# A two-block transformer layer on one core: two buffers for the squares of the first norm, memory attention's keys and values in another pool, norm 2's statistics one step later

## The chip, the core and the metric

The kernel runs on one core of one Trainium2 chip. TensorE (PE) multiplies matrices, VectorE (DVE) and ScalarE (ACT) work on tiles, GpSimd (POOL) does a little of the same, SyncE (SP) issues nearly all transfers. Each engine executes its own instructions in the order in which the program holds them, and waits on semaphores for the others. The metric is the device time of one execution in microseconds (us). Of the kernel before, three runs have a median of 1642.4 us (1641.32 to 1644.54).

## The reference, cut to what matters

Two blocks over a sequence of 512 tokens with 1024 features, everything in float32.

The first block norms x, shifts and scales it by parameters made from a condition vector, and mixes gated linear attention and differential attention; then norm 2 and a gated feed-forward layer:

```python
sh1, sc1, gt1, sh2, sc2, gt2 = adaln_params(c, w_mod, b_mod)   # silu(c) @ w_mod + b_mod
px = project(modulate(x, norm1_g, sh1, sc1), w_in)             # rmsnorm(x) * (1 + sc1) + sh1
mix = concat([gla_merge(...), diff_merge(o, diff_norm_g)]) @ w_out
x = x + gt1 * mix
x = x + gt2 * swiglu(modulate(x, norm2_g, sh2, sc2), w_ffn_in, w_ffn_out)
```

The second block has a pooling and forgetting-attention mixer, attention over 256 memory rows, and a convolved feed-forward layer, each between a norm before and a norm after:

```python
x = x + rms_norm(merged @ w_mix_out, mix_post_g)
x = x + rms_norm(mem_attention(rms_norm(x, xa_pre_g), mem_n, w_xq, w_xkv, w_xo), xa_post_g)
x = x + rms_norm(conv_ffn(rms_norm(x, ffn_pre_g), w_up, conv_w, conv_b, w_down), ffn_post_g)
```

## The kernel before, in words

Features lie on partitions, tokens along the free dimension: X is 8 tiles (k = 0 to 7) of 128 x 512. A float32 product is made of three matmuls of a reduced format: every operand is split into a high part (hi, a cast) and a low part (lo, what the cast left over), and `mm3` (L196 to L198) and `tm_part` (L285 to L287) issue hi·hi, and the two mixed products. `wsplit` (L173) brings a weight tile: an SP transfer into the ring `wf` (2 buffers), the cast into `whi` on ACT (L187), the subtraction into `wlo` on DVE (L188; some on POOL). The feed-forward layers put some of these into memory of their own, named Fhi and Flo.

A scheduler places the instructions of each engine by a priority that counts up with the text; `tc.cur_priority -= n` lets an instruction go earlier, `tc.issue_after(i)` holds it behind instruction i. A tile from a pool waits until what lay at that place, a former buffer of the same tag or a pool that has been closed, is read for the last time.

Three places matter here.

The head. `normed_x` (L427) squares X: for each pair of tiles ACT squares the even one into t (tag sqt0, two buffers), DVE squares the odd one into u (L433, tag sqt1, `bufs=2 - j`, one buffer) and adds t (L434), and PE sums u over partitions (`sum_sq`, L313). `warm` (L488) puts matmuls of no use ahead of these sums: `WU` before the first, `WX` before each later one. Then come the root (L165 to L170), its broadcast (L332, L333), X times it (L441), and per tile `modulated`: hi on ACT (L381), the affine on DVE or POOL (L382), lo (L383). Between them PE makes the condition's parameters (`mod_tiles`, L353, L365). Queries and keys (s, 512 columns a matmul) and the values `gv` (272 columns) follow. `gd` (L1171) is a constant of 128 numbers for the differential attention's norm; it reads `cols`, a tile that SP brings. The context rows have a norm of their own: cX times its root (L424), then hc (L381 to L383).

Norm 2. After the out-projection, `norm2` (L1323) is a generator that runs between the matmul groups of the feed-forward layer, one `yield` for a group's quarter: `W4` steps before the second half of the tokens has its statistics (L313), then 3 steps until they are broadcast. X's first tiles get the projection added at L1343.

Memory attention. Keys and values, KV, lie in the pool `xp`, which is closed when the attention is done. `post` (L1434) writes the output projection into KV's place (L1438), norms it there (L1452) and adds it to X (L1453); `after` runs between matmul groups as norm 2 does, `rbp` is its broadcast root. The convolved feed-forward layer then takes the memory of the closed pool for Fhi, Flo, z and others: what is put there waits until KV has been read for the last time, at L1453. `hq` is a pool that stays open to the end.

Of the kernel before, what the change touches and what calls it, by code (L numbers as in the profile page):

```python
# [10 lines left out]
F32 = mybir.dt.float32  # L11
# [3 lines left out]
ALU = mybir.AluOpType  # L15
# [5 lines left out]
S = 512  # L21
TT = S // 128
CTX = 256
MEM = 256
# [22 lines left out]
QP = (0,)  # L47
Q3 = 0
MG = 1
WU, WX, WW = 15, 1, 5  # L50
MV, W0 = (0, 1), 1
XG = 9
ML = 0
W4, W5 = 1, 1
W1, W2 = 2, 2
X2 = (0, 2, 4)
XR, DR = (1, 3, 5, 7), (1, 3, 5, 7)
# [3 lines left out]
WO = 50  # L61
# [19 lines left out]
def kernel(ctx: ExitStack, tc: tile.TileContext, a: dict, out: bass.AP, stop=None):  # L81
    nc = tc.nc
    V, G, A, T = nc.vector, nc.gpsimd, nc.scalar, nc.tensor

    def f32(ap):
        return ap.bitcast(F32)
# [20 lines left out]
    def mis(dt=F32):  # L107
        return ps.tile([128, 512], dt, tag="mis", name="mis")
# [18 lines left out]
    def col(name, i):  # L127
        o = COLS[name][0] + i
        return cols[:, o:o + 1]
# [180 lines left out]
    def sum_sq(pt, sq, start, stop):  # L310

        for t in range(sq.shape[-1] // 128):
            ins = T.matmul(pt[:, 32 * t:32 * t + 32], sq[:, t * 128:(t + 1) * 128], ones, start=start and t == 0, stop=stop,  # L313
                           skip_group_check=True).ins
        return ins

    def fm_stats(pool, sq, name):

        n = sq.shape[-1] // 128
        pt = mis()  # L320
        sum_sq(pt, sq, True, True)
        return rms(pool, pt, n, name)

    def rms(pool, pt, n, name):
        return rsqrt(pool, pt[:, :32 * n].rearrange("p (t o) -> p t o", o=32)[:, :, 0], n, 1.0 / D, name)

    def bcast(dst, r):

        n = r.shape[-1]
        pb = mis()  # L330
        for t in range(n):
            T.matmul(pb[:, t * 128:(t + 1) * 128], r[:, t:t + 1].to_broadcast([128, 128]), ident, start=True, stop=True)  # L332
        return A.copy(dst, pb[:, :n * 128]).ins  # L333
# [43 lines left out]
    def modulated(t, hi, lo, sc, sh, pool, tag, eng=G):  # L377

        n = t.shape[-1]
        u = pool.tile([128, n], F32, tag=tag, name=tag, bufs=2)  # L380
        hi_at[0] = A.activation(hi, t, AF.Identity, scale=sc, bias=sh).ins  # L381
        eng.tensor_scalar(u, t, sc, sh, ALU.mult, ALU.add)  # L382
        return V.tensor_tensor(lo, u, f32(hi), ALU.subtract).ins  # L383
# [5 lines left out]
    with tc.tile_pool(name="st", bufs=1) as st, tc.tile_pool(name="st2", bufs=2) as st2:  # L389
# [37 lines left out]
        def normed_x(x):  # L427

            pt = mis()
            for k in range(0, KT, 2):  # L430
                t, u = (st2.tile([128, S], F32, tag=f"sqt{j}", name="sqt", bufs=2 - j) for j in range(2))
                A.activation(t, x[:, k], AF.Square)
                V.tensor_tensor(u, x[:, k + 1], x[:, k + 1], ALU.mult)  # L433
                V.tensor_tensor(u, u, t, ALU.add)  # L434
                with tc.issue_after(warm(WU if k == 0 else WX)):
                    last_warm[0] = sum_sq(pt, u, k == 0, k == KT - 2)
            yield
            rb = st.tile([128, S], F32, tag="rbx", name="rbx")
            yield bcast(rb, rms(st, pt, TT, "x"))
            for k in range(KT):  # L440
                V.tensor_tensor(x[:, k], x[:, k], rb, ALU.mult)  # L441
                if k == 1:
                    yield
            yield
# [26 lines left out]
        def hidden(k0):  # L471
            affine(scx, "norm1_g", 8, 0, k0, 2)
            for k in range(k0, k0 + 2):
                ins = modulated(X0[:, k], hhi[:, k], hlo[:, k], scx[:, k:k + 1], mods[:, k, 0:1], st, "mx", V if k in MV else G)
            return ins
# [8 lines left out]
        def warm(n, ins=None):  # L484

            for _ in range(n):
                with (tc.issue_after(ins or last_warm[0]) if ins or last_warm[0] else ExitStack()):
                    last_warm[0] = T.matmul(pq[:, :128], ident, ident, start=True, stop=True).ins  # L488
            return last_warm[0]
# [10 lines left out]
        hid = hidden(0)  # L500
# [667 lines left out]
        mnl = mlo[:, 4:8].rearrange("p k (u t) -> p (k u) t", u=2)  # L1168

    gd = midp.tile([128, 1], F32, name="gd")  # L1170
    V.tensor_scalar(gd, col("diff_norm_g", 0), 0.8, None, ALU.mult)  # L1171

    def mem_in(k):
        m = ap2.tile([128, MEM], F32, tag="mk", name="mk")
# [116 lines left out]
    sp = ctx.enter_context(tc.tile_pool(name="sp", bufs=2))  # L1291
# [31 lines left out]
    def norm2(x, y):  # L1323
        for _ in range(W4 if x else W5):
            yield
        r = fm_stats(sp, sqs[:, x:y], "n2")
        for _ in range(3 if x else 1):
            yield
        bcast(rb[:, x:y], r)
        for k in range(KT):  # L1330
            if k % 2:
                yield
            t = sp.tile([128, S // 2], F32, tag="n2t", name="n2t")
            V.tensor_tensor(t, X[k][:, x:y], rb[:, x:y], ALU.mult)
            modulated(t, h2[0][:, k, x:y], h2[1][:, k, x:y], sc2[:, k:k + 1], mods[:, 24 + k, 0:1], sp, "n2u")

    with tc.tile_pool(name="wo", bufs=1) as wo:
        keep = kept(wo, (0, 1, -1, -1, -1), 0)
        have = {(m, 0): wsplit(a["w_out"][m].rearrange("p k m -> p (k m)"), 1024, None, keep()) for m in (3, 4)}
        for m, (p, whi, wlo) in enumerate(parts):  # L1340
            mm3(p, whi[:, 896:1024], wlo[:, 896:1024], mhi[:, 7], mlo[:, 7], False, True)
        for m, (p, _, _) in enumerate(parts):
            V.scalar_tensor_tensor(X[m], p, mods[:, 16 + m, 0:1], X[m], ALU.mult, ALU.add)  # L1343
        for m in range(len(parts)):
            add_sq(X[m], m, 0, S)
        fm(a["w_out"], range(3, KT), KT, lambda k: mhi[:, k], lambda k: mlo[:, k], accs, ev_out, HALVES, after=norm2,
           keep=keep, have=have)
# [86 lines left out]
    def post(Y, gname, nextg, g2, tails, spread):  # L1434


        def ev(m, x, y, p):
            V.tensor_scalar(Y(m // 2 * 2, x, y)[:, m % 2], p, col(gname, m), None, ALU.mult)  # L1438
            add_sq(p, m, x, y)

        def after(x, y):
            rbp = sp.tile([128, S // 2], F32, tag="rbp", name="rbp")
            r = fm_stats(sp, sqs[:, x:y], "post")
            yield
            bcast(rbp, r)
            yield
            rb2 = rbp.rearrange("p (o t) -> p o t", o=1).to_broadcast([128, 2, S // 2])
            held = hq.tile([128, 2, S // 2], F32, tag="hld", name="hld")
            for k in range(0, KT + 2, 2):
                if k < KT:  # L1450
                    y2, x2 = Y(k, x, y), XT[k // 4][:, k % 4:k % 4 + 2, x:y]
                    V.tensor_tensor(y2, y2, rb2, ALU.mult)  # L1452
                    V.tensor_tensor(x2, x2, y2, ALU.add)  # L1453
                    for j in (k, k + 1):
                        A.activation(g2[0][:, j, x:y], X[j][:, x:y], AF.Copy, scale=col(nextg, j))
                    t = held if k == 0 else sp.tile([128, 2, S // 2], F32, tag="sqx", name="sqx", bufs=1)
                    A.activation(t, x2, AF.Square)
                    yield
                if k > 0:
                    for j in (k - 2, k - 1):  # L1460
                        V.scalar_tensor_tensor(g2[1][:, j, x:y], X[j][:, x:y], col(nextg, j), f32(g2[0][:, j, x:y]),
                                               ALU.mult, ALU.subtract)
                    if k > 2:
                        V.tensor_tensor(held, held, last, ALU.add)
                    yield
                if k < KT:
                    last = t

            def tail():
                pt = sums()  # L1470
                for j in range(2):
                    sum_sq(pt, held[:, j], j == 0, j == 1)
                r = rms(sp, pt, (y - x) // 128, "pre")
                if spread:
                    bcast(rb[:, x:y], r)
                return r
            tails[x] = tail
        return ev, after
# [203 lines left out]
    hq = ctx.enter_context(tc.tile_pool(name="hq", bufs=1))  # L1682
    xa = ExitStack()
    xp = xa.enter_context(tc.tile_pool(name="xp", bufs=1))
    xt = xa.enter_context(tc.tile_pool(name="xt", bufs=2))
    KV = xp.tile([128, 8, MEM], F32, name="KV")
    KVM, VM = KV[:, 0:4], KV[:, 4:8].rearrange("p (t u) n -> p t (u n)", t=2)
    g4 = new_q()
    Ym = xp.tile([128, KT, S], F32, name="Ym")
# [5 lines left out]
    if stop == "x3":  # L1695
        return finish()
    nc.sync.dma_start(KV, kvd)
    xh = hp.tile([128, 8, S], F32R, tag="hhi", name="xh")
# [52 lines left out]
    def head_step(i):  # L1751
        if next(heads[i], heads) is heads:
            heads.pop(i)
    ev, after = post(lambda k, x, y: KV[:, k:k + 2] if x else Ym[:, k:k + 2, x:y], "xa_post_g", "ffn_pre_g", g4, rb_of, True)
    xk = kept(xp, (-3, -2, -1, 2), NF)
# [216 lines left out]
```

## Time and profile before

| | us |
|---|---|
| median of three runs | 1642.4 |
| the profiled execution | 1641.52 |
| its span, first to last instruction | 1639.1 |
| PE busy | 1590.6 |
| DVE busy | 948.0 |
| ACT busy | 718.7 |

The profiled execution has 2.4 us around its span. Its mean granted clock of TensorE is 0.989 of full speed. A busy PE is not always a fast one: where the granted clock is 0.5, a matmul counts as busy for longer. The rows of the trace that are used further down name the stretch by its time from the span's start.

### The profile page before, as it was taken

How to read it: one execution, taken by the hardware profiler on the slowest of the kernel's cores; microseconds unless marked ns; L12 is line 12 of the kernel's file. 1: busy time of each engine (PE TensorE's matmuls, PEld its weight loads, DVE VectorE, ACT ScalarE, POOL GpSimd, SP SyncE). 2: the span in 40 equal slices, each digit the busy share in tenths (PEclk: the TensorE clock that was granted, in tenths of full speed). 3: DMA queues.
4: the chain of work that ended last, by engine and by line, in shares of the span. 5: the costliest groups of instructions: out<-in, count | busy, mean ns of one | idle time of the engine just before them, and what ended most of it. 6: DMA issues, size and time to landing. Idle time of an engine off the chain costs nothing.

```text
span 1639.1 us, 25459 instructions
## 1 busy us (share of the span) xinstructions
PE 1590.6 (97%) x10098; PEld 1355.6 (83%) x10098; DVE 948.0 (58%) x1791; ACT 718.7 (44%) x1353; POOL 214.1 (13%) x237
## 2 busy tenths in 40 slices
PE   7999999999999999999999999999998999999997
PEld 5798977778889888888889777888988988888887
DVE  5626898788765222223335676445788777776333
ACT  3424555677645323232223565224466544444221
POOL 0300000111022122210004000122000222221001
PEclk8999999999999999999999999999999999999999
DMA  8232245332322333333332212234211233323332
GB/s 350 82 89 78 66 158 180 124 100 78 128 88 78 103 94 99 91 99 94 93 114 72 77 39 65 91 103 148 84 52 34 83 93 100 103 90 97 97 93 74
DMA packets 49046, 163.23 MB, mean 100 GB/s; under 512 B 5664, under 2 KB 11296, under 8 KB 47392
## 3 DMA queue, kind: packets, MB, share of 16 engines
q1 hardware_dynamic: 45328, 158.15, 30.4%
q10 hardware_dynamic: 3312, 3.18, 0.6%
q8 instruction: 79, 1.29, 0.3%
q0 software_dynamic: 288, 0.28, 0.1%
q14 instruction: 39, 0.32, 0.1%
HBM read 158.72 MB, written 3.15 MB: 99 GB/s over the span
## 4 chain that ended last, share of the span: by engine, by line
PE 85%; DVE 5%; ACT 3%; DMA 1%; issue 1%; POOL 0%; ACTq 0%; DVEq 0%; POOLq 0%
PE acc L197 16%; PE acc L198 16%; PE acc L196 16%; PE s L198 5%; PE s L196 5%; PE s L197 5%; PE acc L286 3%; PE acc L285 3%; PE acc L287 3%; PE mis L1147 1%; PE mis L1632 1%; DVE wlo L188 1%; PE acc L775 1%; PE s L1118 1%; DMA mk<-in_memT 1%
## 5 line engine op out<-in xcount | busy, mean ns | idle before, releaser
L187 ACT CAST whi<-wf 128x1024 fp32r<-128x1024 f32 (+4 forms) x221 | 228.6, 1034 | 422.6 <-PE acc L197 277.7
L188 DVE TENSOR_TENSOR wlo<-wf,whi 128x1024 fp32r<-128x1024 f32 (+2 forms) x183 | 222.0, 1213 | 176.2 <-ACT whi L187 172.3
L196 PE MATMUL acc<-qhi,whi 128*128 128x512 f32 (+1 forms) x640 | 239.4, 374 | 0.0
L197 PE MATMUL acc<-qlo,whi 128*128 128x512 f32 (+1 forms) x640 | 239.3, 374 | 0.0
L198 PE MATMUL acc<-qhi,wlo 128*128 128x512 f32 (+1 forms) x640 | 239.3, 374 | 0.0
L196 PEld LDWEIGHTS acc<-qhi,whi 128*128 128x128 f32 x640 | 120.8, 189 | 19.6
L197 PEld LDWEIGHTS acc<-qlo,whi 128*128 128x128 f32 x640 | 120.7, 189 | 19.7 <-issue 0.2
L198 PEld LDWEIGHTS acc<-qhi,wlo 128*128 128x128 f32 x640 | 120.7, 189 | 19.3
L196 PE MATMUL s<-qhi,whi 128*128 128x512 f32 (+1 forms) x336 | 128.3, 382 | 0.0
L198 PE MATMUL s<-qhi,wlo 128*128 128x512 f32 (+1 forms) x336 | 128.3, 382 | 0.0
L197 PE MATMUL s<-qlo,whi 128*128 128x512 f32 (+1 forms) x336 | 128.2, 382 | 0.0
L188 POOL TENSOR_TENSOR wlo<-wf,whi 128x1024 fp32r<-128x1024 f32 x38 | 91.0, 2396 | 214.3 <-ACT whi L187 214.3
L1417 DVE TENSOR_TENSOR e<-e,s 128x512 f32<-128x512 f32 (+1 forms) x22 | 14.3, 651 | 154.2 <-PE s L198 154.1
L197 PE MATMUL acc<-glo,whi 128*128 128x512 f32 (+1 forms) x208 | 74.4, 358 | 0.1
L196 PE MATMUL acc<-ghi,whi 128*128 128x512 f32 (+1 forms) x208 | 74.4, 358 | 0.0
L198 PE MATMUL acc<-ghi,wlo 128*128 128x512 f32 (+1 forms) x208 | 74.2, 357 | 0.0
L196 PEld LDWEIGHTS s<-qhi,whi 128*128 128x128 f32 x336 | 64.0, 190 | 11.9
L197 PEld LDWEIGHTS s<-qlo,whi 128*128 128x128 f32 x336 | 64.0, 190 | 11.8
L198 PEld LDWEIGHTS s<-qhi,wlo 128*128 128x128 f32 x336 | 63.9, 190 | 11.8
L197 PE MATMUL acc<-Flo,whi 128*128 128x512 f32 (+1 forms) x187 | 71.6, 383 | 0.0
L285 PE MATMUL acc<-whi,hhi 128*128 128x256 f32 (+1 forms) x224 | 67.1, 299 | 3.4 <-ACT qsq L654 2.5
L286 PE MATMUL acc<-wlo,hhi 128*128 128x256 f32 (+1 forms) x224 | 65.6, 293 | 3.3 <-DVE wlo L188 3.3
(648 smaller groups left out, 3833.4 us busy)
## 6 DMA issues: line engine op xcount, KB each, us to landing
wf<-in_w_ffn_in SPq DMA_DIRECT2D x44, 512.0 KB, 3.6
wf<-in_w_up SPq DMA_DIRECT2D x44, 512.0 KB, 3.5
wm<-in_w_mod SPq DMA_DIRECT2D x32, 512.0 KB, 3.6
wm<-in_w_mod SPq DMA_DIRECT2D x8, 1024.0 KB, 11.7
wf<-in_w_ffn_out SPq DMA_DIRECT2D x16, 512.0 KB, 3.5
wf<-in_w_g SPq DMA_DIRECT2D x16, 512.0 KB, 3.5
wf<-in_w_down SPq DMA_DIRECT2D x16, 512.0 KB, 3.5
wf<-in_w_dv SPq DMA_DIRECT2D x8, 512.0 KB, 3.7
```

The lines of the kernel that those rows point to most:

```text
L187: A.copy(hi[:, :n], wf[:, :n])
L188: (lo_eng or V).tensor_tensor(lo[:, :n], wf[:, :n], f32(hi[:, :n]), ALU.subtract)
L196: T.matmul(o, lhi, rhi, start=start, stop=False)
L197: T.matmul(o, lhi, rlo, start=False, stop=False)
L198: ins = T.matmul(o, llo, rhi, start=False, stop=stop).ins
L285: T.matmul(o, bhi(k), whi, start=k == 0, stop=False)
L286: T.matmul(o, bhi(k), wlo, start=False, stop=False)
L287: T.matmul(o, blo(k), whi, start=False, stop=k == KT - 1)
L775: T.matmul(p[32 * j:32 * j + 32, :256], silc[:, 4 * kc + j], wf[:, j * 256:(j + 1) * 256], start=kc == 0, stop=kc == 1, skip_group_check=T ...
L1118: T.matmul(s_[:, n0:n1], QF[:, c, ts], KA[:, c, n0:n1], start=True, stop=False)
L1147: T.matmul(p[:, :128], aT[:, kt * 128:(kt + 1) * 128], v, start=kt == 0, stop=kt == NKT - 1)
L1632: T.matmul(pO[:, ts], vz[:, kt, hp_, 64 * e:64 * e + 128], pT[:, kt * 128:(kt + 1) * 128], start=kt + e == 0, stop=kt - t + e == 1, skip_g ...
```

## The change

```diff
-WU, WX, WW = 15, 1, 5
+WU, WX, WW = 13, 1, 5
...
-W4, W5 = 1, 1
+W4, W5 = 2, 1
...
             for k in range(0, KT, 2):
-                t, u = (st2.tile([128, S], F32, tag=f"sqt{j}", name="sqt", bufs=2 - j) for j in range(2))
+                t, u = (st2.tile([128, S], F32, tag=f"sqt{j}", name="sqt", bufs=2) for j in range(2))
...
     gd = midp.tile([128, 1], F32, name="gd")
-    V.tensor_scalar(gd, col("diff_norm_g", 0), 0.8, None, ALU.mult)
+    with tc.issue_after(hid):
+        V.tensor_scalar(gd, col("diff_norm_g", 0), 0.8, None, ALU.mult)
...
         r = fm_stats(sp, sqs[:, x:y], "n2")
-        for _ in range(3 if x else 1):
+        for _ in range(2 if x else 1):
             yield
...
         for m, (p, _, _) in enumerate(parts):
+            tc.cur_priority -= 2 * WO
             V.scalar_tensor_tensor(X[m], p, mods[:, 16 + m, 0:1], X[m], ALU.mult, ALU.add)
+            tc.cur_priority += 2 * WO
...
         def after(x, y):
-            rbp = sp.tile([128, S // 2], F32, tag="rbp", name="rbp")
+            rbp = sp.tile([128, S // 2], F32, tag="n2t", name="rbp")
...
-    KV = xp.tile([128, 8, MEM], F32, name="KV")
+    KV = hq.tile([128, 8, MEM], F32, name="KV")
```

The first norm has 13 useless matmuls ahead of its first sum in place of 15, two buffers for u, and the product gd is held behind the first tiles' low parts (`hid`). In norm 2 the second half's statistics come a step later and the broadcast a step sooner after them, so the broadcast keeps its place; X's additions at L1343 have a higher priority. KV lies in `hq`; `rbp` shares the buffers of norm 2's tile `n2t`. Nothing that is computed changes. The transfers of SP stand in the same order as before; the order of other engines changes in three stretches.

In the head, DVE's rows for the squares and their sums (sqt is t and u, identr a copy of the identity, X_97 the input):

```order
 L434 TENSOR_TENSOR sqt<-sqt 128x512
-L125 CAST identr<-ident 128x128
-L1171 TENSOR_SCALAR gd<-cols 128x1
 L433 TENSOR_TENSOR sqt<-X_97 128x512
 L434 TENSOR_TENSOR sqt<-sqt 128x512
-L433 TENSOR_TENSOR sqt<-X_97 128x512
-L434 TENSOR_TENSOR sqt<-sqt 128x512
-L433 TENSOR_TENSOR sqt<-X_97 128x512
-L434 TENSOR_TENSOR sqt<-sqt 128x512
+L125 CAST identr<-ident 128x128
+L433 TENSOR_TENSOR sqt<-X_97 128x512 x2
+L434 TENSOR_TENSOR sqt<-sqt 128x512 x2
```

gd no longer stands among the squares, and the last two odd tiles are squared one right after the other.

Later in the head, DVE's rows after the context's root r_c (wlo of 128x1088 is the second tile of gv's weights):

```order
 L170 SCALAR_TENSOR_TENSOR r_c<-t_c,y_c 128x2
+L188 TENSOR_TENSOR wlo<-wf,whi 128x1088
 L424 TENSOR_TENSOR cX<-cX,rbc 128x256 x8
-L383 TENSOR_TENSOR hc<-mc,hc 128x256 x8
-L188 TENSOR_TENSOR wlo<-wf,whi 128x1088
```

The weights' low part moves ahead of sixteen context instructions. On PE, the matmuls of gv that stood among the last query and key matmuls now stand behind all of them.

In norm 2, twelve feed-forward matmuls that stood behind the second half's sum on PE now stand ahead of it. On ACT and DVE one more weight tile (Fhi, Flo) stands ahead of the root that follows.

At the end of memory attention, ACT's rows of the kernel before, from the last squares of the output projection on:

```order
L1311 ACTIVATE sqt<-acc 128x256 x7
L165 ACTIVATE y_post<-mis,epsc 128x2
L167 ACTIVATE y_post<-y_post 128x2
L333 COPY rbp<-mis 128x256
L165 ACTIVATE y_pre<-sums,epsc 128x2
...
L333 COPY rb<-mis 128x256
L1455 ACTIVATE qhi<-X_5343,cols 128x256 x2
L1457 ACTIVATE sqx<-X_5343 128x512
L187 CAST Fhi<-wf 128x1024
```

And of the changed kernel, where each line number from 1172 on is higher by one to three:

```order
L1312 ACTIVATE sqt<-acc 128x256 x6
L187 CAST Fhi<-wf 128x1024
L1312 ACTIVATE sqt<-acc 128x256
L187 CAST Fhi<-wf 128x1024
L165 ACTIVATE y_post<-mis,epsc 128x2
L167 ACTIVATE y_post<-y_post 128x2
L165 ACTIVATE y_pre<-sums,epsc 128x2
L167 ACTIVATE y_pre<-y_pre 128x2
L333 COPY rbp<-mis 128x256
L333 COPY rb<-mis 128x256
```

The first two casts into Fhi move from behind all of X's updates to ahead of the norm's root, and on DVE the two Flo move with them. Both broadcasts (rbp and rb) now stand together. Later in this stretch ACT has one table load more: between the two functions of the second half's root y_pre stands now a gelu, with loads on either side.

## Rows read from the trace of the kernel before

**Rows 1.** The page's part 1: busy time, share of span, instructions.
```profile
PE 1590.6 (97%) x10098; PEld 1355.6 (83%) x10098; DVE 948.0 (58%) x1791; ACT 718.7 (44%) x1353; POOL 214.1 (13%) x237
```
**Rows 2.** Busy time by stretch, with granted clock and share of DMA.
```profile
core 0: us, PE busy (x) PEld busy (x) DVE busy (x) ACT busy (x) POOL busy (x), PEclk, DMA share, GB/s
0.00:20.00 20.00, 13.25 (x80) 12.05 (x84) 8.26 (x16) 4.69 (x8) 1.29 (x10) 0.81 0.91 355
20.00:75.00 55.00, 48.70 (x316) 35.12 (x309) 36.49 (x86) 26.97 (x52) 16.44 (x17) 0.91 0.52 193
...
67.00:75.00 8.00, 5.10 (x28) 4.88 (x27) 6.15 (x11) 2.87 (x7) 1.66 (x3) 0.79 0.22 70
...
480.00:500.00 20.00, 17.82 (x138) 17.64 (x137) 14.84 (x32) 11.92 (x23) 6.85 (x7) 0.91 0.41 132
1250.00:1300.00 50.00, 44.33 (x340) 43.05 (x339) 37.07 (x86) 30.26 (x57) 8.67 (x19) 0.93 0.21 64
```
**Rows 3.** PE's waits over the span: us in total, times, longest us.
```profile
PE mis L313 <- DVE sqt L434: 4.9, 3, 2.6
```
**Rows 4.** DVE in the head: start, us, line, operation, out<-in, count [idle before <-releaser].
```profile
6.06 0.68 DVE L434 TENSOR_TENSOR sqt<-sqt 128x512 f32<-128x512 f32 x1
9.40 0.15 DVE L1171 TENSOR_SCALAR gd<-cols 128x1 f32<-128x1 f32 x1 [2.52 <-DMA cols<-in_cols]
12.16 0.69 DVE L433 TENSOR_TENSOR sqt<-X 128x512 f32<-128x512 f32 x1 [1.17 <-PE mis L313]
```
**Rows 5.** PE in the head: the second and last sums, the first product.
```profile
11.05 1.08 PE L313 MATMUL mis<-ones,sqt 128*128 128x32 f32 x8 [2.60 <-DVE sqt L434]
...
17.20 1.92 PE L313 MATMUL mis<-ones,sqt 128*128 128x32 f32 x8 [1.00 <-DVE sqt L434]
...
26.60 0.51 PE L196 MATMUL s<-hhi,whi 128*128 128x512 f32 x1 [0.86 <-ACT hhi L381]
```
**Rows 6.** SP's issue of condition weights, and transfers to 80 us (median to landing).
```profile
3.76 1.01 SPq L402 DMA_DIRECT2D wm<-in_w_mod  x2
...
wm<-in_w_mod SPq DMA_DIRECT2D x8, 1024.0 KB, 11.7
X<-in_xT SPq DMA_DIRECT2D x4, 512.0 KB, 5.1
```
**Rows 7.** PE and DVE where the values' second weight tile is due.
```profile
70.38 0.41 PE L286 MATMUL acc<-wlo,hhi 128*128 128x272 f32 x1 [2.90 <-DVE wlo L188]
...
59.02 0.16 DVE L170 SCALAR_TENSOR_TENSOR r_c<-t_c,y_c 128x2 f32<-128x2 f32 x1
...
69.04 1.28 DVE L188 TENSOR_TENSOR wlo<-wf,whi 128x1088 fp32r<-128x1088 f32 x1
```
**Rows 8.** PE and DVE at L1343 and in norm 2.
```profile
454.16 0.36 PE L196 MATMUL acc<-mhi,kh 128*128 128x256 f32 x1 [1.88 <-DVE X L1343]
...
489.27 0.60 PE L313 MATMUL mis<-ones,sqs 128*128 128x32 f32 x4 [2.18 <-DVE sqs L1312]
...
453.27 0.75 DVE L1343 SCALAR_TENSOR_TENSOR X<-acc,mods,X 128x512 f32<-128x512 f32 x1
...
491.14 1.23 DVE L188 TENSOR_TENSOR Flo<-wf,Fhi 128x1024 fp32r<-128x1024 f32 x1 [0.77 <-ACT Fhi L187]
```
**Rows 9.** PE and ACT where the convolved feed-forward layer begins.
```profile
1266.84 0.58 PE L196 MATMUL s<-qhi,Fhi 128*128 128x256 f32 x1 [4.50 <-ACT Fhi L187]
...
1268.10 0.58 PE L198 MATMUL s<-qhi,Flo 128*128 128x256 f32 x1 [0.46 <-DVE Flo L188]
...
1288.96 0.71 PE L332 MATMUL mis<-ident,r_pre 128*128 128x128 f32 x4 [0.71 <-DVE r_pre L170]
...
1265.74 1.04 ACT L187 CAST Fhi<-wf 128x1024 fp32r<-128x1024 f32 x1 [0.97 <-DVE X L1453]
...
1285.24 1.28 ACT L165 ACT_TABLE_LOAD   x1
1286.54 0.26 ACT L165 ACTIVATE y_pre<-sums,epsc 128x2 f32<-128x2 f32 x1
```

## The prediction

> **What bounds the kernel now.** The page's part 1 comes first: PE is busy for 97% of the span [rows 1], so the time is PE's own work plus what it waits or runs slowly for. 1639.1 - 1590.6 leaves 48.5 us of idle time, and a change that removes no matmul can give back that and the slow clock, no more. Second, the table of PE's waits says where the idle time is: the sums of the first norm, which wait for the squares, hold 4.9 us of it in three waits [rows 3]; the next are single waits of 4.50, 2.90, 2.18 and 1.88 us [rows 7 to 9]. Third, the table by stretch gives the clock there [rows 2]. [...] The change touches all these waits, so I take them one by one.
>
> **Squares of the first norm.** Before, u has one buffer: from the third pair on, the square at L433 waits for PE's sum of the pair before (the first such wait is 1.17 us), and ahead of the second pair DVE stood 2.52 us for a tile that only gd needs [rows 4]. So DVE and PE take turns, and the last sum ends at 17.20 + 1.92 = 19.12 [rows 5]. Afterwards gd stands behind X's products and u has two places. DVE is done with the first pair at 6.06 + 0.68 = 6.74; three pairs are left, six instructions at 0.69 us [rows 4], so the last u stands at about 11.1 with the cast of the identity between. The input does not hold it up: a quarter of X takes 5.1 us to land, and all four are issued ahead of the transfer that SP issues at 3.76 [rows 6]. The last sum takes 1.08 us at the high clock or 1.92 at the low one [rows 5]; with the latter it ends at 12.8 to 13. From the last sum to the first product, 26.60 - 19.12 = 7.5 us pass, through root, parameters and broadcast [rows 5]; that chain is not changed. Gain: 19.1 - 12.8 = 6.3 us. The far ends: 7, if the sums run at the high clock; and 3.6, if the parameters' weights set the pace. Their first transfer is issued at 3.76 and the median of eight takes 11.7 us to land [rows 6]: 15.5, against 12.8 for the sums, is 2.7 us lost. I take it near the upper end, since the first of eight that queue up lands sooner than the median one. The two useless matmuls less cost nothing: they lie in the wait for u.
>
> The later weights of the head are issued sooner as well, since the buffers they wait for come free sooner; the transfers run at a share of 0.91 in the first 20 us but only 0.52 from 20 to 75 [rows 2], so there is room.
>
> **The values' second weight tile.** PE waits 2.90 us for wlo, which DVE begins only at 69.04, behind the context's products [rows 7]. In the new order it stands right behind r_c, which is done at 59.2 [rows 7]: ten us sooner, and PE needs it later than before, since all queries and keys now come first. That removes 2.90 us and most of the low clock that follows (3.4 us at it from 67 to 75, 1.6 us lost [rows 2]). Given back: the values' matmuls no longer fill PE's time while the last tiles' low parts are made; I put that at 0.7 us, between 0 (the keys suffice) and 3 (as long a wait as the one removed). Context products and the evacuation of queries now share DVE later, 36.49 of 55 us busy [rows 2]; it has the room. Gain 3.8 us, 1.5 to 4.5.
>
> **L1343.** PE waits 1.88 us for X [rows 8]. The update moves past one low part, but the one directly ahead of the last X stays there. 0, between a loss of 0.8 (one X instruction, 0.75 us [rows 8], ahead of a weight that is needed) and a gain of 1.9.
>
> **Norm 2.** PE stands 2.18 us before the second half's sum [rows 8]. Twelve matmuls now go first: at 44.33 us for 340 instructions, 0.13 us each [rows 2], they fill 1.5 us. With 0.7 us of idle time left, the clock should stay up: at 0.91 over 20 us [rows 2], 1.8 us are lost to it now, some 1.4 of them behind this wait. On the other side a Flo of 1.23 us [rows 8] stands ahead of the root, and PE reaches the broadcast sooner, with 24 matmuls (3.1 us) between. I take a gain of 2.2, half the clock's part; 2.9 at most, and a loss of 0.5 if the root comes late.
>
> **KV.** PE's longest wait, 4.50 us, is for Fhi, and ACT's cast of it waits for X at L1453, the last reader of KV, in whose memory Fhi lies [rows 9]. In `hq`, KV gives nothing to Fhi, and two casts and two low parts go ahead of the root. Behind the wait come 0.46 us for Flo and 0.71 us for r_pre [rows 9], and the low clock: 0.93 over 50 us is 7 us at it, some of them idle [rows 2]; I count 2.0 us. Together 7.7 us. What is late next: Fhi (1.04 us) and Flo stand ahead of the root, so the broadcast comes about a us later, and the second half's low parts, which DVE makes between the first half's z and its taps, set the pace. DVE is busy 37.07 of 50 us [rows 2], nearly all of the middle of it. I give back 2.2 us for both. Gain 5.5; at least the 2.0 that the two low parts of 1.23 us, now earlier, take from DVE's queue; at most 7.7. KV's own transfer stands at the same place of SP's queue and costs nothing.
>
> One table load more stands in the second half's root. Here a load takes 1.28 us and the next instruction begins 0.02 us after its end [rows 9]. From the sums to r_pre there are then two loads, a gelu and five small instructions, about 4.0 us, under 56 matmuls (7.3 us at 0.13). It is hidden. [...]
>
> **Sum.** 6.3 + 3.8 + 0 + 2.2 + 5.5 = 17.8 us off the profiled execution's 1641.5: 1623.7. The median of the runs lies 0.9 above that execution: 1624.6, say 1625. Nothing between these stretches takes it back, since PE is the bound there too and every wait is against ACT or DVE, which move with it.
>
> **Rivals.** First: the head gives less. If the weights set its pace (3.6) and the values gain only 1.5, 5.1 us come in place of 10.1: 1630. For it speaks the DMA share of 0.91 up to 20 us [rows 2]; against, that the first weights are the first in the queue.
>
> Second: the convolved layer's start is bound by DVE. Then only 2.0 of 5.5 us come, and norm 2's clock still drops (0.8 in place of 2.2): 1625 + 3.5 + 1.4 = 1630. With the first rival too, 1635. DVE's share there speaks for it; but PE has a weight tile's 24 matmuls three times over to go on with.
>
> Third, KV and norm 2 do nothing, because another tile of the closed pool still holds Fhi back, or the root replaces the sum as what is late: 1625 + 7.7 = 1633. Against it, the releaser is L1453 alone [rows 9].
>
> Fourth, slower: the clock stays at its low level through the queries and keys. From 20 to 75 us PE is busy 48.70 us at 0.91 [rows 2], that is 44 us of work at the high clock; all of it at the low one would lose 44 us where 5 are lost now. The change is lost when about 18 more us of that work run low, slower by 0.2% at 21. The waits between sums, after which the clock has fallen here to a mean of 0.81 in the first 20 us [rows 2], become shorter, which speaks against it; the useless matmuls are fewer, which speaks for it. At 22 us of such work the time would be 1647. [...]
>
> **Chances.** The forecast (1620 to 1628): 0.56. Still more, below 1620: 0.08, down to 1617 where every part is at its upper end. First and second rival, apart or together: 0.22. Third: 0.06. Several of these together, to within 0.2%, about what can be told from no change here (3.3 us): 0.05. Fourth: 0.03. So faster 0.92, the same 0.05, slower 0.03. Range 1618 to 1636, which leaves some 0.15 out on both sides.
>
> **What would show it.** In the new profile, the last sum of the first norm ends near 13 us and the first query product begins near 20; no wait of PE for wlo near 60 to 65; the sum of norm 2 waits under 1 us with the clock at 1 behind it; PE goes from the broadcasts of the last root into Fhi without a wait, and some waits for qlo appear 6 to 14 us later. The wait at L1343 stays near 1.9 us. I am wrong if the first product still begins after 23 us, or if PE's idle time around the convolved layer's start is as long as before under other names.

## The result, and the profile after

The changed kernel takes 1624.04 us (median of four runs, 1622.92 to 1624.92), beside 1643.06 us for four runs of the kernel before (1641.32 to 1644.54). The ratio is 0.9883, interval 0.9868 to 0.9899: 19 us less, between 17 and 22. The forecast was 1625 in a range of 1618 to 1636. The sum came out, but not each of its terms: one was too large and three too small. The ratios here and below leave out executions in a slower state, two of over 5 ms among them (one of the kernel with norm 2's edit alone, one of before), so they need not be the quotient of the medians beside them.

The profiled execution took 1624.87 us with a span of 1623.0, which is 16.1 us shorter than before. These 16.1 us are what is divided up below; the rest of the 19 is that before's profiled execution was one of its faster ones and after's one of its slower ones.

The page's part 1 of the kernel after (busy time, share of span, instructions), for [rows 1]:

```profile
PE 1584.7 (98%) x10094; PEld 1349.6 (83%) x10094; DVE 946.6 (58%) x1791; ACT 718.5 (44%) x1354; POOL 211.5 (13%) x237
```

PE's idle time is 1623.0 - 1584.7 = 38.3 us, 10.2 less than before, and its busy time is 5.9 less though only four records of 10098 are gone, those of the two useless matmuls less (a useless matmul leaves two records: x30 before for 15, x26 now for 13). Nearly all of that part I put down to the clock, whose mean over the span is 0.994 here and 0.989 before. The table by stretch of the kernel after (columns as in [rows 2]) shows where:

```profile
core 0: us, PE busy (x) PEld busy (x) DVE busy (x) ACT busy (x) POOL busy (x), PEclk, DMA share, GB/s
0.00:20.00 20.00, 16.42 (x90) 14.60 (x90) 8.76 (x19) 5.06 (x9) 1.29 (x10) 0.76 0.90 344
...
60.00:75.00 15.00, 15.00 (x122) 15.00 (x121) 11.52 (x26) 9.30 (x20) 5.82 (x8) 1.00 0.18 55
...
470.00:490.00 20.00, 19.54 (x162) 19.19 (x161) 16.22 (x37) 13.67 (x26) 8.55 (x9) 1.00 0.45 130
...
1234.00:1284.00 50.00, 48.58 (x392) 47.44 (x391) 39.68 (x88) 31.55 (x58) 7.19 (x17) 1.00 0.24 75
```

The values' end, norm 2 and the start of the convolved layer stand at 8 to 14 us earlier times than in [rows 2]. Where the clock was 0.79, 0.91 and 0.93 it is now 1.00, and PE is idle for 0, 0.46 and 1.42 us. The first 20 us went the other way: 0.81 before, 0.76 now.

PE's waits after (us in total, times, longest), for [rows 3] and the waits in [rows 7 to 9]:

```profile
PE acc L196 <- DVE X L1345: 1.8, 1, 1.8
PE mis L313 <- DVE sqt L434: 1.7, 2, 0.9
...
PE acc L196 <- DVE z L1793: 1.4, 1, 1.4
PE acc L775 <- DMA wm<-in_w_mod: 1.3, 2, 0.9
...
PE acc L286 <- DVE wlo L188: 0.4, 1, 0.4
PE mis L313 <- DVE sqs L1313: 0.3, 1, 0.3
```

The waits of 4.50 for Fhi and 2.90 for wlo are gone (the 0.4 for wlo is another, later wait, which before had too), and the 2.18 for sqs is down to 0.3. New are the wait for z at L1793 and a few of under 0.5 us.

PE's rows in the head of the kernel after (columns as in [rows 4, 5]), and the first context product:

```profile
7.32 0.98 PE L313 MATMUL mis<-ones,sqt 128*128 128x32 f32 x8
...
9.49 1.10 PE L313 MATMUL mis<-ones,sqt 128*128 128x32 f32 x8 [0.90 <-DVE sqt L434]
10.41 0.78 PE L488 MATMUL s<-ident 128*128 128x128 f32 x2
11.98 1.92 PE L313 MATMUL mis<-ones,sqt 128*128 128x32 f32 x8 [0.80 <-DVE sqt L434]
13.71 0.77 PE L488 MATMUL s<-ident 128*128 128x128 f32 x2
14.27 1.75 PE L313 MATMUL mis<-ones,sqt 128*128 128x32 f32 x8
...
23.89 0.50 PE L196 MATMUL s<-hhi,whi 128*128 128x512 f32 x1 [0.86 <-ACT hhi L381]
...
72.06 0.28 PE L285 MATMUL acc<-whi,hc 128*128 128x256 f32 x1
```

The last sum no longer waits for its squares: it waits for PE, which makes the third sum, one useless matmul (two records) and itself at the low clock, 0.50 from 11.98 to 16.02. It ends at 16.02, 3.1 us before the 19.12 of [rows 5], and the first product begins 2.7 us sooner. DVE in the same stretch of the kernel after:

```profile
7.95 0.69 DVE L433 TENSOR_TENSOR sqt<-X 128x512 f32<-128x512 f32 x1 [0.83 <-DMA X<-in_xT]
...
10.63 0.69 DVE L433 TENSOR_TENSOR sqt<-X 128x512 f32<-128x512 f32 x1 [0.46 <-PE mis L313]
11.24 1.28 DVE L434 TENSOR_TENSOR sqt<-sqt 128x512 f32<-128x512 f32 x2
```

Its last u stands at 12.52: it waited 0.83 us for X, whose quarters take 6.7 us to land in this execution (median) and 5.1 in [rows 6], and 0.46 for the sum that frees the second buffer.

PE's rows after at L1343 (L1345 now), in norm 2 and at the convolved layer's start, beside [rows 8, 9]:

```profile
447.10 0.36 PE L196 MATMUL acc<-mhi,kh 128*128 128x256 f32 x1 [1.77 <-DVE X L1345]
...
481.79 0.60 PE L313 MATMUL mis<-ones,sqs 128*128 128x32 f32 x4 [0.31 <-DVE sqs L1313]
...
1252.71 0.28 PE L196 MATMUL s<-qhi,Fhi 128*128 128x256 f32 x1
...
1275.04 0.61 PE L332 MATMUL mis<-ident,r_pre 128*128 128x128 f32 x4
1278.87 0.50 PE L196 MATMUL acc<-qhi,whi 128*128 128x512 f32 x1 [1.42 <-DVE z L1793]
```

By these points the 16.1 us divide so: up to the first product 2.7; from there to the first context product 5.5 (53.7 us before, 48.2 now); from there to L1343, where nothing was changed, 1.2 lost; norm 2 to its broadcast 3.0; from there to the convolved feed-forward layer's first Fhi 0.5 lost, counted with that wait left out; from there to the end 6.5 gained, the new wait already taken off.

### The profile page after: what moved, and what is told of

Its sections match the earlier page's. It is cut to its first block, busy times and chain, and to the rows that moved or that the text cites. A ratio compares the mean times of both kernels' runs of the same rounds, so it can differ in the third digit from the quotient of the medians.

```text
span 1623.0 us, 25451 instructions
## 1 busy us (share of the span) xinstructions
PE 1584.7 (98%) x10094; PEld 1349.6 (83%) x10094; DVE 946.6 (58%) x1791; ACT 718.5 (44%) x1354; POOL 211.5 (13%) x237
## 4 chain that ended last, share of the span: by engine, by line
PE 84%; DVE 6%; ACT 4%; DMA 3%; issue 2%; POOL 1%; SPq 0%; ACTq 0%; DVEq 0%; POOLq 0%
PE acc L197 16%; PE acc L196 16%; PE acc L198 16%; PE s L196 5%; PE s L198 5%; PE s L197 5%; PE acc L285 2%; PE acc L286 2%; PE acc L287 2%; DVE wlo L188 1%; PE mis L1635 1%; PE mis L1147 1%; ACT whi L187 1%; PE acc L775 1%; DMA wf<-in_w_out 1%
## 5 line engine op out<-in xcount | busy, mean ns | idle before, releaser
L196 PEld LDWEIGHTS s<-qhi,whi 128*128 128x128 f32 x336 | 63.1, 188 | 11.8
L197 PEld LDWEIGHTS s<-qlo,whi 128*128 128x128 f32 x336 | 63.1, 188 | 11.8
```

Source lines behind the costliest of these rows:

```text
L196: T.matmul(o, lhi, rhi, start=start, stop=False)
L197: T.matmul(o, lhi, rlo, start=False, stop=False)
```

## The experiments

Gains in us are the ratio times the median of the runs of before beside it. A kernel "on before" has one part of the change alone, "on after" is the changed kernel with one edit.

**The head's three edits, on before.**

```diff
-WU, WX, WW = 15, 1, 5
+WU, WX, WW = 13, 1, 5
...
-                t, u = (... bufs=2 - j) for j in range(2))
+                t, u = (... bufs=2) for j in range(2))
...
+    with tc.issue_after(hid):
         V.tensor_scalar(gd, col("diff_norm_g", 0), 0.8, None, ALU.mult)
```

> The kernel before with the edits of the first norm alone: 13 useless matmuls in place of 15, two buffers for u, gd held back. The values' second weight tile moves with them on DVE, ahead of the context rows. Theory: the head's two terms are independent of the other edits, so the shift that the changed kernel shows at the first context product (80.31 to 72.06, 8.2 us) comes whole: 1643 - 8 = 1635, minus or plus 1.5; the sums end 3 us sooner and the wait for wlo at 70 is gone. Rival: half of that shift needs the other edits or is lost later to the transfers of the modulation weights at L775; then 1638 to 1640.

Measured: 1633.95, ratio 0.9933 (0.9911 to 0.9954), 11 us. The last sum ends at 15.22, the first product begins at 22.29 and the first context product at 71.68. The head and the values are thus about half of the change (8.2 of the 16.1 us in the profile), and they don't need the rest of it. The four parts tried alone add up to 22.7 us (11, 8.5, 3.0 and 0.2) beside 19, each with an interval of some 2 to 4 us to either side. Which of the three edits it is, the next two say; the two matmuls less were not tried alone on before.

**The second buffer alone, on before** (the `bufs=2` line of the diff above).

> The kernel before with one edit: u has two buffers (15 useless matmuls and gd as before). Theory: the second buffer alone makes DVE and PE overlap, and it alone moves the values' second weight tile ahead of the context rows, so nearly all of the 8 to 10 us of the three edits together come from it: 1635. gd then still stands in front of the last two squares and costs at most 0.5 us. Rival: gd's wait for its transfer, 2.52 us in the trace of before, is a gain of its own: 1638.

Measured: 1634.55, ratio 0.9952 (0.9933 to 0.9971), 7.9 us. The first product begins at 21.55, the context products at 70.27; PE's wait for wlo is gone, so the move of the values' weight tile comes with this line alone. DVE now waits 1.61 us for the transfer of `cols` at gd, the step that the other edit takes out.

**gd held alone, on before** (the `issue_after` of the same diff).

> The kernel before with gd held back and nothing else. Theory: with one buffer for u, DVE then waits for PE's sum in place of the transfer; the second sum comes up to 2.4 us sooner, the third and fourth follow PE and DVE in turns, and the last ends 2 us sooner: 1642. wlo stays behind the context rows and its wait of 2.9 us stays. Rival: gd is most of the head's gain: 1637.

Measured: 1642.33, ratio 0.9992 (0.998 to 1.0003): no difference that can be told. DVE in the head of this kernel:

```profile
8.91 0.69 DVE L433 TENSOR_TENSOR sqt<-X 128x512 f32<-128x512 f32 x1 [1.96 <-PE mis L313]
...
12.20 0.69 DVE L433 TENSOR_TENSOR sqt<-X 128x512 f32<-128x512 f32 x1 [1.81 <-PE mis L313]
...
15.70 0.69 DVE L433 TENSOR_TENSOR sqt<-X 128x512 f32<-128x512 f32 x1 [2.01 <-PE mis L313]
```

Of the 2.52 us of [rows 4] the most come back at the same place, as 1.96 us of waiting for PE's first sum, since there is one buffer. The second square begins 0.6 us sooner (8.91 beside 9.51), and so does the second sum (10.45 beside 11.05), but in this execution that sum takes 1.72 us, at a clock of 0.67 from 10 to 12 us, in place of 1.08 at 1.00, and the third starts at 13.74 as before (13.71). So the buffer let through 0.6 us at most, and the clock took those; the last sum still starts at 17.24.

**The values' second weight tile first, on before.**

```diff
-        tc.cur_priority -= WO
+        gw = WO + (100 if n == 1088 else 0)
+        tc.cur_priority -= gw
...
-        tc.cur_priority += WO
+        tc.cur_priority += gw
```

> The kernel before with a higher priority for the casts and low parts of the values' weights alone; the second low part then stands ahead of the eight hc but behind seven of cX. Squares as before. Theory: the wait of 2.9 us at 70 and the low clock behind it go, 4 us: 1640. Rival: PE waits somewhere else for what DVE now does later (hc, or the evacuation of queries), and nothing is gained: 1644.

Measured: 1639.63, ratio 0.9973 (0.9962 to 0.9984), 4.4 us (2.6 to 6.2). PE no longer waits for wlo, and from first product to first context product 47.5 us pass in place of 53.7, as in the changed kernel (48.2). This term was in the order of the weight tile, not in a faster head: the first product begins at 27.93 here.

**KV's pool, on before.**

```diff
-            rbp = sp.tile([128, S // 2], F32, tag="rbp", name="rbp")
+            rbp = sp.tile([128, S // 2], F32, tag="n2t", name="rbp")
...
-    KV = xp.tile([128, 8, MEM], F32, name="KV")
+    KV = hq.tile([128, 8, MEM], F32, name="KV")
```

> The kernel before with KV in the pool that stays open and rbp under norm 2's tag, nothing else. Theory: the 4.50 us wait for Fhi, 0.46 for Flo and 0.71 for r_pre go, with the low clock behind them, and 1.4 us come back as a wait for z: 6 to 7 us, 1636.5. Rival: DVE sets the pace of this stretch and only the two low parts' 2.4 us come: 1640.5.

Measured: 1635.43, ratio 0.9948 (0.9928 to 0.9969), 8.5 us (5.1 to 11.8); its profiled span is 6.5 shorter. The waits for Fhi, Flo and r_pre are gone, and PE's waits have the one for z here too:

```profile
PE acc L196 <- DVE z L1790: 1.4, 1, 1.4
```

So what is given back belongs to this edit, and it is not what the prediction named. The two lines, rbp's buffers and KV's pool, were not tried apart.

**Norm 2 a step later, on before** (`W4, W5 = 2, 1` and `range(2 if x else 1)`).

> The kernel before with W4 = 2 and two steps in place of three, nothing else. Theory: 12 matmuls fill 1.5 us of the wait of 2.18 and the clock stays high behind it, 3 us in all: 1640. Rival: the clock falls all the same, or the root comes late at the broadcast: 1641.5 to 1643.

Measured: 1642.32 beside 1644.26, ratio 0.9982 (0.9966 to 0.9998), 3.0 us (0.3 to 5.6). The stretch and PE's row in this kernel:

```profile
480.00:500.00 20.00, 19.42 (x161) 19.07 (x161) 16.04 (x34) 13.11 (x26) 8.60 (x8) 1.00 0.45 137
```

```profile
488.83 0.60 PE L313 MATMUL mis<-ones,sqs 128*128 128x32 f32 x4 [0.32 <-DVE sqs L1312]
```

The wait falls from 2.18 to 0.32, and the clock that was 0.91 in [rows 2] is 1.00.

**L1343's priority, on before** (the two lines of the diff around it).

> The kernel before with the higher priority of X's update at L1343 alone. Theory: on DVE only the update and one low part change places, the wait for the last X stays at 1.8 to 1.9 us: no difference, 1643. Rival: the wait shrinks by the 0.75 us of one update, 1642.3, below what the timing tells, but seen in the trace.

Measured: 1643.24, ratio 0.9999 (0.9985 to 1.0014). PE waits 1.76 us there. It does nothing, as forecast.

**Four useless matmuls between the sums, on after.**

```diff
-WU, WX, WW = 13, 1, 5
+WU, WX, WW = 13, 4, 5
```

> The changed kernel with four useless matmuls ahead of each later sum in place of one. It tests whether the low clock from 11 to 21 us costs the head its missing three us. Theory: the sums end when the last square does, the three more matmuls a sum lie in PE's waits, and if they keep the clock high the last two sums and the parameters after them take 1.0 us each in place of 1.9: 1621 to 1622, first product near 21.5 in place of 23.9. Rival: the clock falls all the same, and nine more matmuls of 0.21 us at the low clock stand in the way: 1625 to 1627.

Measured: 1622.11, ratio to before 0.9869 (0.9852 to 0.9886). The first 20 us and PE's rows in them:

```profile
0.00:20.00 20.00, 16.83 (x137) 14.75 (x137) 11.98 (x25) 8.45 (x15) 1.29 (x10) 1.00 0.91 351
```

```profile
6.90 1.08 PE L313 MATMUL mis<-ones,sqt 128*128 128x32 f32 x8
...
12.36 0.98 PE L313 MATMUL mis<-ones,sqt 128*128 128x32 f32 x8
13.27 1.07 PE L353 MATMUL acc<-wm,silc 128*32 128x256 f32 x16
...
19.39 0.49 PE L196 MATMUL s<-hhi,whi 128*128 128x512 f32 x1 [0.86 <-ACT hhi L381]
```

With four matmuls between the sums PE is busy for all of the 4 us from 10 to 14, and the clock stays at 1.00; the last sum ends at 13.34 and the first product begins at 19.39. These are the times that the prediction gave for the changed kernel (near 13, near 20). Of the 4.5 us gained up to the first product the whole time shows some 2 us; the two intervals overlap.

The edit changes the order on DVE too, so this run alone does not test the clock. With four matmuls the scheduler has DVE square and add pair by pair; no square waits for PE, as the last one does in the changed kernel (0.46 us), and the third u is done at 9.77, without the last square ahead of it:

```profile
9.08 0.69 DVE L434 TENSOR_TENSOR sqt<-sqt 128x512 f32<-128x512 f32 x1
```

What the clock does with the order unchanged, the next table shows.

**The changed kernel once more, and with 15 useless matmuls ahead of the first sum, on after** (`WU` 13 as it is, and 15).

> The changed kernel, word for word, as the measure for the three others of this set: 1624. Theory: where the low clock begins in the head and when X and the modulation weights land differs from run to run, so its trace need not show the sums' end at 16.0 us again, but 14 to 16; the waits at the convolved layer's start are the same to 0.1 us.

> The changed kernel with 15 useless matmuls ahead of the first sum, as before the change. Theory: the two matmuls lie in PE's wait for the first u or 0.5 us beyond it, and the engine is busier up to 8 us; the clock stays high a little longer, and the time is the same to 1 us: 1623 to 1625. Rival: the first sum starts 0.7 us later and the head with it: 1625.

Measured: again 1624.24 (1623.37 to 1628.96), ratio 0.9883 (0.9866 to 0.9899); with 15, 1621.35 (1620.57 to 1623.77), ratio 0.9862 (0.9847 to 0.9877). On the first 20 us all kernels with two buffers can be set side by side:

| useless matmuls, first and later sums | kernel | granted clock, 0 to 20 us | first product at |
|---|---|---|---|
| 13, 1 | after | 0.76 | 23.89 |
| 13, 1 | head's edits on before | 0.83 | 22.29 |
| 13, 1 | after, once more | 0.83 | 22.17 |
| 13, 1 | z first (below) | 0.91 | 20.23 |
| 15, 1 | second buffer on before | 0.91 | 21.55 |
| 15, 1 | after with 15 | 0.91 | 20.33 |
| 13, 4 | after with 4 | 1.00 | 19.39 |
| 13, 4 | with 4 and z first (below) | 1.00 | 19.52 |

With gd out of the way (all rows but the fifth, where DVE waits 1.61 us for `cols`) the first product goes with the clock, from 23.89 at 0.76 to 19.39 at 1.00. Not all of that is the clock: in the first row X landed late, and the third sum begins at 11.98, in the other rows of the same order at 10.73 to 11.20. Counted from the third sum, in that order, the first product comes after 11.91 us at 0.76, 11.09 at 0.83 (both rows) and 9.47 and 9.50 at 0.91. So the clock is worth 2.4 of the 3.7 us between the first and the fourth row, and the later third sum, behind the wait of 0.83 us for X, the other 1.25. With z first the last sum ends near 13 without the extra matmuls:

```profile
11.95 0.98 PE L316 MATMUL mis<-ones,sqt 128*128 128x32 f32 x8
```

With four matmuls between the sums the clock stays at 1.00 over the first 20 us, in both executions that have them. Whether two more ahead of the first sum do anything is not settled: the two executions with 15 had 0.91, but one of the four with 13 had it too, and the times of whole runs overlap.

**z ahead of a weight tile, on after.**

```diff
+    behind, first_z = [None], [None]
...
-        (lo_eng or V).tensor_tensor(lo[:, :n], wf[:, :n], f32(hi[:, :n]), ALU.subtract)
+        with (tc.issue_after(behind[0]) if behind[0] else ExitStack()):
+            (lo_eng or V).tensor_tensor(lo[:, :n], wf[:, :n], f32(hi[:, :n]), ALU.subtract)
...
+            behind[0] = first_z[0] if i == NP + 1 else None
             fm(w, [i], KT, bhi, blo, alloc, ev)
+            behind[0] = None
...
-                V.tensor_tensor(z[:, 2 + x:2 + y], p, rb[:, x:y], ALU.mult)
+                zi = V.tensor_tensor(z[:, 2 + x:2 + y], p, rb[:, x:y], ALU.mult).ins
+                if x and g and first_z[0] is None:
+                    first_z[0] = zi
```

> The changed kernel, in which the low part of the second full-width weight tile is held on DVE behind the first two z of the second half. In the changed kernel that low part took 2.24 us in place of 1.23, while POOL made another one (2.39 us), and PE waited 1.42 us for the z behind it. Theory: z is made when its root's broadcast lands, the wait of 1.4 us goes, and the low part, now after POOL's, takes 1.2 us: 1622.6. Rival 1: a low part of DVE takes 2.2 us here whatever POOL does. Rival 2: PE waits as long for that low part or for the next z: 1624.

Measured: 1625.93, ratio 0.9884 (0.9869 to 0.9899), the same as the changed kernel and not the 1622.6 that was expected. PE's wait for z is gone, and from the broadcast of r_pre to the end 346.84 us pass; in the four kernels of the changed order without this edit it is 347.96 to 348.11. So in the traces the 1.4 us wait was worth 1.2, which the time of a whole run can't show. DVE and POOL in the changed kernel:

```profile
1275.01 2.39 POOL L188 TENSOR_TENSOR wlo<-wf,whi 128x1024 fp32r<-128x1024 f32 x1 [5.00 <-ACT whi L187]
...
1276.24 2.24 DVE L188 TENSOR_TENSOR wlo<-wf,whi 128x1024 fp32r<-128x1024 f32 x1 [1.74 <-ACT whi L187]
1278.40 0.41 DVE L1793 TENSOR_TENSOR z<-acc,rb 128x256 f32<-128x256 f32 x1
```

and with z first:

```profile
1272.92 2.40 POOL L191 TENSOR_TENSOR wlo<-wf,whi 128x1024 fp32r<-128x1024 f32 x1 [4.98 <-ACT whi L189]
1274.46 0.43 DVE L1798 TENSOR_TENSOR z<-acc,rb 128x256 f32<-128x256 f32 x1 [2.04 <-ACT rb L336]
...
1275.13 1.27 DVE L191 TENSOR_TENSOR wlo<-wf,whi 128x1024 fp32r<-128x1024 f32 x1
```

In the changed kernel the low part lies ahead of z on DVE and takes 2.24 us while POOL makes another; behind z, when POOL is all but done, it takes 1.27.

**Both of the last two edits, on after** (`WX` 4 and z first).

> The changed kernel with four useless matmuls ahead of each later sum of the first norm, and with z ahead of the low part. Theory: the two gains are in different places and add: 4.5 us of clock in the head at most and 1.4 us at z, 1618 to 1620. Rival: the head's gain is the luck of one run, since the clock's fall moves from run to run, and only z's 1.4 us are left: 1622.6.

Measured: 1620.59 (1619.77 to 1622.28), ratio 0.9856 (0.9839 to 0.9872). The first product begins at 19.52, and 346.31 us pass from r_pre's broadcast to the end. It has the lowest median of all. Against the changed kernel beside it, 1624.24, that is 3.7 us, and the intervals still overlap a little. The two traces of these kernels have 2.7 us up to the first product (22.17 to 19.52) and 1.8 from r_pre's broadcast to the end (348.11 to 346.31). That the two gains add is thus likely but not shown: the profiled span, 1619.2 us, is no shorter than the 1618.9 with four matmuls alone.

## Why the prediction was right, and where it was not

| term | forecast | changed kernel's profile | alone on before |
|---|---|---|---|
| squares, to the first product | 6.3 | 2.7 | with the values 11 (7 to 15) |
| values' weight tile | 3.8 | 5.5 | 4.4 (2.6 to 6.2) |
| L1343 | 0 | 0.1 shorter wait | 0.2 (-2.3 to 2.5) |
| norm 2 | 2.2 | 3.0 | 3.0 (0.3 to 5.6) |
| KV | 5.5 | 6.5 | 8.5 (5.1 to 11.8) |

That the sum came out is in part luck. In the profile the squares fell 3.6 us short of their term and the other three came 3.5 us over theirs (1.7, 0.8 and 1.0); the 17.8 us became 16.1 by the 1.2 and 0.5 us lost in between, and the runs' medians lie 19 us apart. The 3.4 and 7 us at the low clock, which the terms of the values and of KV use, take that level as half of the high one: before's trace reads 0.50 from 72 to 74 us and from 1266 to 1272 and 1.00 from 66 to 70, and in [rows 5] a sum takes 1.08 us at 1.00 and 1.92 at 0.50.

**Squares: mechanism right, size wrong.** The second buffer ended the taking of turns. But the step "the last u stands at about 11.1, the last sum ends at 12.8 to 13" put the last sum right behind the last u. It left out that PE, which had waited for DVE before, would now be behind it: the third sum, a useless matmul and the fourth follow one another at the low clock (0.50) from 11.98 to 16.02. DVE added 1.4 us, with the two waits shown, of which the one for X was put at nothing. By the prediction's own test (first product after 23 us) this step failed in the profiled execution; in the next one of the same kernel the first product began at 22.17. The clock was counted only in the one sum at the end, and the chain from there to the first product was taken over from before at 7.5 us: it takes 7.87 here and 6.05 with four matmuls. With a higher clock over the first 20 us the forecast times come out, with four matmuls (13.34 and 19.39 at 1.00) and nearly so with z first in the changed order (12.93 and 20.23 at 0.91).

**The useless matmuls "cost nothing".** Not shown either way, as said above. The reason given, that they lie in the wait for u, leaves out what such matmuls can do: with four of them between the sums the clock was 1.00 over the first 20 us, with one 0.76 to 0.91.

**Values: right, too small, and the excess is not the change's.** The order's move took the 2.90 us and the low clock from 67 to 75 us (0.79 before; 1.00 from 60 to 75 now), as forecast. In the 8 us from the first product on the clock also rose, from 0.79 to 1.00, some 1.7 us that no term held. The change did not make this rise: the run with gd held alone, with the values in the old order, takes 0.39 to 0.50 us for each query or key matmul from 30 to 32 us, where before takes 0.63 to 0.79 at a clock of 0.50, and the run of the head's edits alone takes 0.63 us for each of seven from 25 to 28 us. Without it the term is about the 3.8 of the forecast, so some 1.7 of the 5.5 are luck of the two executions. The 0.7 us that were to be given back came as a wait of 0.46 for the last tiles' low parts:

```profile
52.66 0.50 PE L197 MATMUL s<-hlo,whi 128*128 128x512 f32 x1 [0.46 <-DVE hlo L383]
```

**Norm 2: right, too small.** The term held 1.5 us of the wait and 0.7 of the clock; 1.9 of the wait came (2.18 to 0.31), and the 1.2 that are left of the 3.0 are put down to the clock (0.91 over 20 us before, 1.00 now).

**KV: right, and what came back was another thing.** Fhi, Flo and r_pre hold PE up no more and the clock is 1.00 over the whole 50 us, 0.93 before. The 2.2 us that were given back ahead of time were 1.42, and for a different reason: not low parts of the second half (there are no such waits 6 to 14 us later), nor the table loads, but z behind a low part that takes 2.24 us on DVE beside POOL's, and 1.27 behind z. ACT's rows at the second half's root in the changed kernel:

```profile
1268.87 1.28 ACT L165 ACT_TABLE_LOAD   x1
1270.17 0.26 ACT L165 ACTIVATE y_pre<-sums,epsc 128x2 f32<-128x2 f32 x1
1270.45 1.28 ACT L1803 ACT_TABLE_LOAD   x1
1271.74 0.42 ACT L1803 ACTIVATE early<-early 128x256 f32<-128x256 f32 x1
1272.18 1.28 ACT L167 ACT_TABLE_LOAD   x1
1273.47 0.20 ACT L167 ACTIVATE y_pre<-y_pre 128x2 f32<-128x2 f32 x1
```

Each instruction begins 0.01 to 0.02 us after the load before it has ended. The last two loads begin 0.02 us after the instruction ahead of them has ended, and PE's broadcast of r_pre at 1275.04 has no wait.

**The 1.2 us lost from the context products to L1343.** No edit touches this stretch. 1.1 of it is the wait for the modulation's weights at L775, 0.2 us before and 1.3 after; other kernels have 0.3 (z first), 1.4 (gd held alone) and 2.1 (the second buffer alone) there, with the old order and the new. I take it as scatter between executions; that was not tried by itself.

**Rivals.** That the weights set the head's pace: no; ahead of the sums stood X, 0.83 us, and the clock, and the run with four matmuls reached 19.39 with the same transfers queued. That DVE binds the convolved layer's start: no, PE is idle 1.42 us of 50. That KV or norm 2 does nothing: no, each gains alone. That the clock stays low through queries and keys: it did sink lower in the first 20 us of this execution, but it was back at 1.00 from 22 us on, before the first product. In other executions it fell for a few us right behind the first product: 0.55 at 24 to 26 us with the second buffer alone, 0.50 there with 15 matmuls on after.

## What to carry to other kernels

When a second buffer ends the taking of turns between two engines, work out the later engine's whole queue again, at the clock that its own waits will leave it; a few useless matmuls between short sums can keep that clock up (here 1.00 over the first 20 us with four of them, 0.76 to 0.91 with one). Removing one wait inside an alternation, without the buffer, brings at most the time until the buffer comes free (here 0.6 of 2.52 us); the rest turns up as a wait for the buffer. Memory of a closed pool makes the next layer's first weights wait for the last reader of the old one (here 4.50 us): look there when the longest wait of TensorE is for a weight that was in memory long before.

## What the runs showed of the hardware

A subtraction of two 128 x 1024 float32 tiles takes 1.23 us on DVE in [rows 8], 1.27 us with z first, and 2.24 us beside the same kind of instruction on POOL, which takes 2.39 us there. In the changed kernel the two lie together for 1275.01 + 2.39 - 1276.24 = 1.16 us, and DVE's takes 1.01 longer: it all but stands still while POOL's runs. The price is nearly the whole overlap; why the one engine holds the other up, these rows don't show.

Which of the two pays is not always DVE. In another stretch of the changed kernel's trace the pair meets in either order:

```profile
851.18 1.07 POOL L1532 TENSOR_TENSOR ws<-u 128x527 f32<-128x527 f32 x1 [7.68 <-DVE u L1526]
851.21 2.12 DVE L188 TENSOR_TENSOR wlo<-wf,whi 128x1024 fp32r<-128x1024 f32 x1
...
867.96 1.23 DVE L188 TENSOR_TENSOR wlo<-wf,whi 128x1040 fp32r<-128x1040 f32 x1
868.04 2.07 POOL L1532 TENSOR_TENSOR ws<-u 128x527 f32<-128x527 f32 x1
```

POOL's begins 0.03 us ahead of DVE's at 851.18, and DVE's takes 2.12; at 867.96 DVE's begins 0.08 us ahead and keeps its 1.23, and POOL's takes 2.07 in place of 1.07. In these rows, as at 1276.24, the one that begins second pays.

The clock in the head was not the same from one execution to the next: four executions with the same 13 and 1 useless matmuls and the same order of the sums had 0.76, 0.83, 0.83 and 0.91 over the first 20 us, and the first product began between 23.89 and 20.23 us, 2.4 us of that by the clock.
